# One core, hybrid streaming trunk: the gate tiles' last square and scaling taken apart, a plain load of h for tile 13, and other rings for the last pair

## The chip, the cores and the metric

The kernel runs on one core of a Trainium2 chip. The metric is device time in microseconds (us). "Before" is the median of three runs. A profiled execution stands beside it: it has its own time, and a span, which runs from its first to its last instruction. Times within the trace count from the start of the span.

## The reference, cut to what matters

One layer (DEPTH is 1) over 2048 prompt frames and 32 sample frames, D = 1024, all in float32:

```python
h = h + jnp.concatenate([yA, yB], axis=-1) @ w_out
gate = jax.nn.sigmoid(rmsnorm(h, g_ple) @ w_ple_gate)
h = h + (p @ w_ple) * gate
y = rmsnorm(h, g_final)
```

yA and yB come from one combined input projection (a gated short convolution and a pooling mixer). The change touches the last two lines alone: the gate's product with what is added to h, and the final norm.

## The kernel before

**Tiles and stages.** The frames are cut into 16 tiles of 128 rows (0 to 15) and one of 32 rows (16); NT is 17. Stage one makes yA and yB and writes them to memory. Stage two makes h = x + y W_out pair by pair and writes it to `h_d`; e = p W_ple of all tiles but the last prompt tile is made around its start and its end, and lies in `e_d`. Stage three, the gate stage, runs over the pairs of tiles (0, 1), (2, 3) ... (12, 13) in a loop (L1828), and then once over the last pair (14, 15) in a function of its own, `last_pair`. The text names a pair by its first tile: pair 12 is the tiles 12 and 13.

**A pair.** Each pair's product (256 rows by 1024 by 1024) is made by `seven` (L273), a Strassen-like scheme of seven half-size products instead of eight. Every half-size product is 12 matmuls on TensorE (PE), since each operand is split into two parts. Three PSUM banks X, Y, Z are used: X = A11 W11, then Y, then X goes on with S2 T2, Z = S1 T1, X goes on with S3 T3, Z goes on with S4 W22, X ends with A22 T4. Between these, `carry` copies a bank to SBUF on ScalarE (ACT), and `out` adds a bank to what was carried, on VectorE (DVE). A bank is written again only when its copy or its addition has been read out of it. `seven` calls steps 1 to 6 between the products, and whatever a step traces stands at that place in the program: step 1 after the first product, 2 after Y, 3 after S2 T2, 4 after S1 T1, 5 after S3 T3, 6 after the one that follows it. The last pair takes S4 W22 ahead of S3 T3, and ends with `end` (two halves of A22 T4, each of 256 columns, L1722).

**After the products.** `out` (L1576) makes the gate by a sigmoid on ACT (L1582, or L1579 for the last quarter), and multiplies e by it on DVE (L1584), a quarter at a time: (0,0), (1,1), (0,1), (1,0), the first figure being the tile of the pair, the second the half of its columns. Is there no h (`h is None`), then h is added by a transfer: GpSimd (POOL) issues a DMA from `h_d` that accumulates onto the tile e in SBUF (L1590), after (0,1) for the first tile and after (1,0) for the second. Then e holds the final h.

**The final norm of a tile** is `done_g` (L1594): a sum of squares on ACT (`sumsq`, L94), two small operations on POOL (L73, L77) that give the factor, a scaling by it and by g on DVE (L1597), and the store of 512 KB to the output (L1600; on POOL's queue up to tile 11, on SP's queue for the tiles 12 to 15). The tiles of a pair are finished in the next pair: the first tile in step 4, the second in step 6. For pair 12 that is in `last_pair`, steps 3 and 4. The last pair itself has h loaded plainly, adds on DVE (`gated`, L1640 and L1641) and norms by `square`, `weigh`, `root` and `normed`.

**What sets the order.** The tile framework orders each engine's instructions when it builds the program, by order in the program and by its own forecast of when their inputs are there; on the chip each engine and each DMA queue runs its list in that order. `keep_in_program_order` (in `last_pair`: `fixed`) pins an instruction behind the one of its engine that was traced just before it; others may still pass both. So the scaling of step 4 stands behind the instruction that VectorE had traced last before step 4.

**Buffers.** `ya` has 5 buffers of 512 KB: the e of every pair, and in the last pair also e of tile 14 and two tiles hg. `xh` has 4: the tiles hn (h turned, for the products of a pair, loaded by quarters) and the last pair's two h. `cmb` has 8: the split operands of the products, and in the last pair the four tiles wl, the weight of p W_ple for tile 15 (`chunk`, step 1), whose product is made inside the last pair (`second`, L109). A load waits until the last user of its buffer is done; for an e whose buffer held a finished tile that is the store of that tile.

Of the kernel before, what the change touches and what calls it, by code (L numbers as in the profile page):

```python
# [15 lines left out]
P = 128  # L16
# [12 lines left out]
NT = SEQ // P + 1  # L29
# [7 lines left out]
def trunk(ctx, tc, x_p, x_s, c_conv, c_pool, p_p, p_s, g_mix, w_in, conv_w, conv_b, pool_w,  # L37
# [8 lines left out]
    h_d = tc.dram_tile([T, D], F32, name="h_d")  # L46
    e_d = tc.dram_tile([T, D], F32, name="e_d")
# [44 lines left out]
    def sumsq(x, n, name, r=None, later=False):  # L92
        ssq = sm.tile([P, 1], F32, tag="ssq", name=f"ssq_{name}")
        ins = nc.scalar.activation(junk[:n], x[:n], AF.Square, accum_out=ssq[:n])  # L94
        if later:
            tc.keep_in_program_order(ins)
        return rstd_of(ssq, n, name, r)
# [295 lines left out]
    def load_rows(pool, name, i, pr, sa=None, queue=nc.sync):  # L393
        r, n = tiles[i]
        t = ring4(pool, f"{name}_{i}")
        queue.dma_start(t[:n], pr[r:r + n] if sa is None else rows_of(pr, sa, r, n))
        return t
# [906 lines left out]
    with ExitStack() as s2:  # L1304
        pool = lambda name, bufs: s2.enter_context(tc.tile_pool(name=name, bufs=bufs, reuse_waits="tile"))
        qa, xh, ya, cmb = (pool(*a) for a in (("qa", 2), ("xh", 4), ("ya", 5), ("cmb", 8)))
# [86 lines left out]
        S, W = {}, {}  # L1393
# [38 lines left out]
        for c in range(EARLY):  # L1432
            if c == EARLY - 2:
# [3 lines left out]
        st, ss = (s2.enter_context(tc.tile_pool(name=name, bufs=bufs, side="right", reuse_waits="tile"))  # L1437
                  for name, bufs in (("st", 4), ("ss", 3)))
# [64 lines left out]
        W = {}  # L1503
# [64 lines left out]
        def gate_ops(h, e, n, name, i):  # L1568
            scale = lambda at: rs_h[:n, i + at[0]:i + at[0] + 1]

            def carry(ps, at):
                t = st.tile([P, NH], F32, tag="t", name=f"c_{name}_{at[0]}{at[1]}")
                carried.append(nc.scalar.copy(t[:n], ps[:n]))  # L1573
                return t

            def out(ps, c, at):  # L1576
                if c is None:
                    c = st.tile([P, NH], F32, tag="t", name=f"g_{name}_{at[0]}{at[1]}")
                    nc.scalar.activation(c[:n], ps[:n], AF.Sigmoid, scale=scale(at))  # L1579
                else:  # L1580
                    nc.vector.tensor_tensor(c[:n], ps[:n], c[:n], op=ALU.add)
                    nc.scalar.activation(c[:n], c[:n], AF.Sigmoid, scale=scale(at))  # L1582
                ee = half_of(e, at, n)
                nc.vector.tensor_tensor(ee, ee, c[:n], op=ALU.mult)  # L1584
                if h is not None:
                    hh = half_of(h, at, n)
                    nc.vector.tensor_tensor(hh, hh, ee, op=ALU.add)
                elif at[0] + at[1] == 1:
                    r = tiles[i + at[0]][0]
                    nc.gpsimd.dma_start(e[at[0]], h_d[r:r + P], accum_op=ALU.add)  # L1590

            return carry, out

        def done_g(i, h, later=False):  # L1594
            r, n = tiles[i]
            rf = sumsq(h, n, f"f{i}", later=later)
            ins = nc.vector.scalar_tensor_tensor(h[:n], h[:n], rf[:n], g_bc[:n], op0=ALU.mult, op1=ALU.mult)  # L1597
            if later:
                tc.keep_in_program_order(ins)
            (nc.sync if NT - 5 <= i < NT - 1 else nc.gpsimd).dma_start(rows_of(y_p, y_s, r, n), h[:n])  # L1600
# [16 lines left out]

            return carry, out

        def last_pair(i, A, sooner, before):  # L1620

            pps = load_pps(ss.tile([P, 2, 2, P], F32R, tag="s", name="pps_l"), i + 1, nc.sync)
            e = load_rows(ya, "e", i, e_d)
            wp = []
            chunk = lambda: wp.extend(load_wp(cmb, "wl", nc.sync))

            h = [load_rows(xh, "h", i + b, h_d) for b in range(2)]
            tt = nc.vector.tensor_tensor
            carry, _ = gate_ops(h, [e], P, f"g{i}", i)
            hg = [ring4(ya, f"hg_{b}") for b in range(2)]
# [64 lines left out]
            def rest():  # L1699
                of_first(cols_of(0), nc.gpsimd)  # L1700
# [33 lines left out]
                weigh(1, cols_of(0))  # L1734
                normed(1, root(1))

            seven(f"g{i}", A, W, held, out, {1: chunk, 3: sooner, 4: lambda: (before(), rest()), 5: upper_half}, first_tile=True, end=end)

        def prep_g(i, ahead=False):

# [48 lines left out]
        S = {}  # L1789
        steps = prep_g(0)  # L1790
# [17 lines left out]
        def short_gate():  # L1808
# [7 lines left out]
            done_g(NT - 1, h)  # L1816
            yield

        def joined(a, b):
            def both(p, q):  # L1820
                def run():
                    p()
                    q()
                return run
            return {**a, **{st: both(a[st], f) if st in a else f for st, f in b.items()}}

        short_steps = short_gate()
        for i in range(0, NT - 3, 2):  # L1828
            A = S.pop(i)
            following = prep_g(i + 2, not i)  # L1830
            e = [load_rows(ya if i else xh, "e", i + b, e_d) for b in range(2)]
            if i:
                following = joined(following, finish)
            seven(f"g{i}", A, W, *gate_ops(None, e, P, f"g{i}", i), following)
            finish = {st: lambda b=b, i=i, e=e: done_g(i + b, e[b], True) for b, st in enumerate((4, 6))}
            if i in (0, 2, 4):
                next(short_steps)
        last_pair(NT - 3, S[NT - 3], finish[4], finish[6])

# [1 line left out]
_INS = ['x_prompt', 'x_sample', 'cache_conv', 'cache_pool', 'p_prompt', 'p_sample', 'g_mix', 'w_in',  # L1841
# [25 lines left out]
```

## Time and profile before

| what | us |
|---|---|
| median of 3 runs | 918.86 (917.51 to 918.87) |
| the profiled execution's own time | 916.35 |
| its span | 914.6 |
| TensorE busy, of the span | 890.8 (97%) |
| VectorE | 695.2 (76%) |
| ScalarE | 452.8 (50%) |
| GpSimd | 166.9 (18%) |
| mean granted TensorE clock | 0.995 |

How to read it: 1.75 us of the profiled execution's own time lie outside its span, and it was 2.51 us faster than the median. TensorE is busy nearly all of the time, so what counts is the idle time that is left on it and what ends each piece of it. In rows of the timeline the first number is the start, the second the length, then engine and line, `out<-in` by the program's names, and in brackets the engine's idle time before the row with what ended it. SPq and POOLq are the queues on which transfers are issued.

### The profile page before, as it was taken

To read this page: it belongs to the slowest core of one execution; us is meant where nothing else is said; L and a number is where in the kernel's file an instruction comes from. 1 tells how busy PE (TensorE), PEld (TensorE's weight loads), DVE (VectorE), ACT (ScalarE), POOL (GpSimd) and SP (SyncE) were. 2 spreads that over 40 slices of the span, in tenths; PEclk is the share of its full clock that TensorE was granted. 3 is DMA by queue.
4 is the path that set the end of the run, shared out by engine and by line. 5 is a ranking of instruction groups with operands and counts; after the bars stand their busy time and mean duration, and the time that the engine had idled before them with its cause. 6 is when DMAs were issued, how large, how long until landed. Compare 5 with 4: busy or idle time off the path is not lost. (4 is left out here: it accounts for less than half of the span.)

```text
span 914.6 us, 12059 instructions
## 1 busy us (share of the span) xinstructions
PE 890.8 (97%) x4110; PEld 718.0 (79%) x4110; DVE 695.2 (76%) x1138; ACT 452.8 (50%) x818; POOL 166.9 (18%) x304
## 2 busy tenths in 40 slices
PE   8999999999999999999999999999999999999995
PEld 6788888888888778877788886888887787768884
DVE  6899789897993788746677679956557967688874
ACT  7744555554443354433343375643435765446454
POOL 2210122222131123100000021211112201213322
PEclk9999999999999999999999999999999999999999
DMA  8155286856699676767754595878668774687975
GB/s 273 55 187 179 75 257 205 246 170 210 195 346 427 152 225 184 239 204 247 242 154 143 185 364 166 263 234 264 228 226 294 274 235 116 150 228 184 270 206 182
DMA packets 116843, 198.51 MB, mean 217 GB/s; under 512 B 13558, under 2 KB 74542, under 8 KB 115885
## 3 DMA queue, kind: packets, MB, share of 16 engines
q1 hardware_dynamic: 92749, 117.38, 40.9%
q0 software_dynamic: 21584, 75.96, 26.6%
q10 hardware_dynamic: 2448, 4.39, 1.3%
q8 instruction: 32, 0.52, 0.2%
q14 instruction: 30, 0.25, 0.1%
HBM read 132.53 MB, written 65.15 MB: 216 GB/s over the span
## 5 line engine op out<-in xcount | busy, mean ns | idle before, releaser
L185 PE MATMUL z_g<-wg,g_S 128*128 128x512 f32 x192 | 46.5, 391 | 1.0 <-ACT c_g L1573 1.0
L185 PE MATMUL z_o<-wo,y_S 128*128 128x512 f32 x192 | 47.4, 389 | 0.0
L646 PE MATMUL x_zab<-B,w_zab_S 128*128 128x512 f32 x192 | 46.8, 391 | 0.4 <-DVE w_zab_S L84 0.4
L185 PE MATMUL x_o<-wo_T,y_S 128*128 128x512 f32 x192 | 46.3, 390 | 0.9 <-DVE c_o L1319 0.9
L646 PE MATMUL z_zab<-B,w_zab_S 128*128 128x512 f32 x192 | 46.7, 390 | 0.0
L185 PE MATMUL x_o<-wo,y 128*128 128x512 f32 x192 | 45.2, 389 | 0.0
L185 PEld LDWEIGHTS z_g<-wg,g_S 128*128 128x128 f32 x192 | 35.8, 188 | 9.5 <-ACT c_g L1573 2.2
L646 PEld LDWEIGHTS x_zab<-B,w_zab_S 128*128 128x128 f32 x192 | 35.8, 188 | 9.1 <-DVE w_zab_S L84 0.9
L185 PEld LDWEIGHTS x_o<-wo_T,y_S 128*128 128x128 f32 x192 | 35.9, 188 | 8.7 <-DVE c_o L1319 1.3
L185 PEld LDWEIGHTS x_o<-wo,y 128*128 128x128 f32 x192 | 36.0, 188 | 7.7
L646 PEld LDWEIGHTS z_zab<-B,w_zab_S 128*128 128x128 f32 x192 | 35.8, 188 | 7.8 <-DVE w_zab_S L84 0.3
L185 PEld LDWEIGHTS z_o<-wo,y_S 128*128 128x128 f32 x192 | 36.0, 188 | 7.5
L646 PE MATMUL x_ch<-B,w_ch_S 128*128 128x512 f32 x168 | 41.9, 392 | 0.0
L646 PE MATMUL x_zbv<-B,w_zbv_S 128*128 128x512 f32 x168 | 40.9, 392 | 0.5 <-ACT zs L986 0.5
L646 PE MATMUL z_zbv<-B,w_zbv_S 128*128 128x512 f32 x168 | 40.4, 390 | 0.0
L646 PE MATMUL z_ch<-B,w_ch_S 128*128 128x512 f32 x168 | 40.4, 389 | 0.0
L646 PEld LDWEIGHTS x_zbv<-B,w_zbv_S 128*128 128x128 f32 x168 | 31.3, 188 | 8.3 <-ACT zs L986 1.0
L646 PEld LDWEIGHTS x_ch<-B,w_ch_S 128*128 128x128 f32 x168 | 31.3, 188 | 7.3 <-issue 0.4
L646 PEld LDWEIGHTS z_ch<-B,w_ch_S 128*128 128x128 f32 x168 | 31.5, 188 | 6.6
L646 PEld LDWEIGHTS z_zbv<-B,w_zbv_S 128*128 128x128 f32 x168 | 31.5, 188 | 6.5
L81 ACT CAST y_S<-y_fS 128x512 fp32r<-128x512 f32 x28 | 17.0, 620 | 26.7 <-PE x_o L185 11.9
L1373 POOL DMA_DIRECT2D gs<-in_w_ple_gate_dram x16 | 11.5, 716 | 88.2 <-DMA g_d<-gs 33.8
(554 smaller groups left out, 2275.1 us busy)
## 6 DMA issues: line engine op xcount, KB each, us to landing
wn<-in_w_in_dram SPq DMA_DIRECT2D x24, 512.0 KB, 4.7
hn<-h_d SPq DMA_DIRECT2D x65, 128.0 KB, 7.4
y<-y_d SPq DMA_DIRECT2D x16, 512.0 KB, 7.0
p_dT<-T POOLq DMA_DIRECT2D x15, 512.0 KB, 5.6
e<-e_d SPq DMA_DIRECT2D x15, 512.0 KB, 7.6
x<-in_x_prompt_dram SPq DMA_DIRECT2D x14, 512.0 KB, 5.9
e<-h_d POOLq DMA_DIRECT2D x14, 512.0 KB, 8.3
B<-p_d POOLq DMA_DIRECT2D x3, 2048.0 KB, 17.0
```

Of the source, the lines that this page charges most:

```text
L81: ins = nc.scalar.copy(hi, src)
L185: nc.tensor.matmul(ps[:n], lhs[:, k, a, :n], w[b][:, k], start=start and k + q == 0, stop=k == KH - 1 and q == 2, skip_group_check=True)
L646: nc.tensor.matmul(ps, lhs[:, k, x], b[:, k, y], start=start and k + q == 0, stop=stop and k == KH - 1 and q == 2, skip_group_check=True)
L1373: ins = nc.gpsimd.dma_start(t, rows[:, :, half * NH:half * NH + NH])
```

## The change

It has three parts. First, `done_g` can take a factor that is already there, and a new function `finishing` makes four steps of the two tiles' ends: square 0, scale 0, square 1, scale 1 (0 and 1 are the tiles of the pair that went before). In the pairs 2 to 12 they stand in the steps 4, 5, 5, 6 of the next pair; before, square and scaling together stood in 4 and 6. Second, pair 12 (`i == NT - 5`) loads h of tile 13, the fourteenth, plainly into a buffer of `xh`; `out` adds to it on VectorE, and the accumulating transfer is made for tile 12 alone. Third, the last pair takes the ends of pair 12 in another order: square 1 (tile 13) in step 1, scale 1 in step 2, square 0 (tile 12) in step 3, scale 0 in step 4; h of tile 15 comes into `ya` instead of `xh`, and e of tile 14 is asked for after both h instead of before.

```diff
-                if h is not None:
+                if h is not None and h[at[0]] is not None:
                     hh = half_of(h, at, n)
                     nc.vector.tensor_tensor(hh, hh, ee, op=ALU.add)
                 elif at[0] + at[1] == 1:
...
-        def done_g(i, h, later=False):
+        def done_g(i, h, later=False, rf=None):
             r, n = tiles[i]
-            rf = sumsq(h, n, f"f{i}", later=later)
+            rf = rf or sumsq(h, n, f"f{i}", later=later)
...
-        def last_pair(i, A, sooner, before):
+        def last_pair(i, A, square0, scale0, square1, scale1):
...
             pps = load_pps(ss.tile([P, 2, 2, P], F32R, tag="s", name="pps_l"), i + 1, nc.sync)
-            e = load_rows(ya, "e", i, e_d)
             wp = []
             chunk = lambda: wp.extend(load_wp(cmb, "wl", nc.sync))
 
-            h = [load_rows(xh, "h", i + b, h_d) for b in range(2)]
+            h = [load_rows(ya if b else xh, "h", i + b, h_d) for b in range(2)]
+            e = load_rows(ya, "e", i, e_d)
...
-            seven(f"g{i}", A, W, held, out, {1: chunk, 3: sooner, 4: lambda: (before(), rest()), 5: upper_half}, first_tile=True, end=end)
+            seven(f"g{i}", A, W, held, out, {1: lambda: (chunk(), square1()), 2: scale1, 3: square0, 4: lambda: (scale0(), rest()), 5: upper_half}, first_tile=True, end=end)
...
+        def finishing(i, out):
+            steps = []
+            for b in range(2):
+                rf = {}
+
+                def square(b=b, rf=rf):
+                    rf[0] = sumsq(out[b], P, f"f{i + b}", later=True)
+
+                def scale(b=b, rf=rf):
+                    done_g(i + b, out[b], True, rf[0])
+
+                steps += [square, scale]
+            return steps
...
             e = [load_rows(ya if i else xh, "e", i + b, e_d) for b in range(2)]
+            h = [None, load_rows(xh, "h", i + 1, h_d)] if i == NT - 5 else None
             if i:
-                following = joined(following, finish)
-            seven(f"g{i}", A, W, *gate_ops(None, e, P, f"g{i}", i), following)
-            finish = {st: lambda b=b, i=i, e=e: done_g(i + b, e[b], True) for b, st in enumerate((4, 6))}
+                for at, f in zip((4, 5, 5, 6), finish):
+                    following = joined(following, {at: f})
+            seven(f"g{i}", A, W, *gate_ops(h, e, P, f"g{i}", i), following)
+            finish = finishing(i, e if h is None else [e[0], h[1]])
             if i in (0, 2, 4):
                 next(short_steps)
-        last_pair(NT - 3, S[NT - 3], finish[4], finish[6])
+        last_pair(NT - 3, S[NT - 3], *finish)
```

## The prediction

> **What bounds the kernel now.** I read the page's first part, then what TensorE waited for in the gate stage, then busy time by stretches (columns: PE, PEld, DVE, ACT, POOL, granted clock, DMA share, GB/s).
>
> ```profile
> span 914.6 us, 12059 instructions
> PE 890.8 (97%) x4110; PEld 718.0 (79%) x4110; DVE 695.2 (76%) x1138; ACT 452.8 (50%) x818; POOL 166.9 (18%) x304
> ...
> PE x_gl L337 <- DVE c_gl L1608: 2.3, 1, 2.3
> PE x_g L1722 <- DVE c_g L1677: 2.0, 1, 2.0
> PE e L109 <- ACT eout L167: 2.0, 1, 2.0
> PE x_g L185 <- DVE c_g L1581: 1.4, 2, 0.9
> PE z_g L185 <- ACT c_g L1573: 1.0, 1, 1.0
> ...
> 843.00:862.40 19.40, 19.40 (x86) 15.76 (x85) 17.23 (x24) 11.50 (x20) 5.90 (x8) 1.00 1.04 264
> 862.40:881.70 19.30, 19.30 (x86) 15.68 (x85) 16.15 (x23) 10.47 (x19) 5.34 (x8) 1.00 0.78 228
> ```
>
> TensorE is the bound. In the pairs 10 and 12 (the two stretches) it is busy 19.40 of 19.40 and 19.30 of 19.30 us: there no other engine's work costs anything until it is late for a product. What the change can win is TensorE's idle time. Leaving out the 2.0 of e L109, which lies ahead of the pairs, the list sums to 2.3 + 2.0 + 1.4 + 1.0 = 6.7 us. Two of these waits stand in the last pair:
>
> ```profile
> 889.41 0.69 DVE L1640 TENSOR_TENSOR c_g<-e,c_g 128x512 f32<-128x512 f32 x1 [0.79 <-ACT c_g L1673]
> 890.14 0.69 DVE L1641 TENSOR_TENSOR h<-h,c_g 128x512 f32<-128x512 f32 x1
> 893.12 1.06 ACT L94 ACTIVATE junk<-e 128x1024 bf16<-128x1024 f32 x1 [2.26 <-DMA e<-h_d]
> 894.18 0.57 ACT L1573 COPY c_g<-z_g 128x512 f32<-128x512 f32 x1
> 894.80 3.01 PE L185 MATMUL z_g<-wg,g_S 128*128 128x512 f32 x12 [0.99 <-ACT c_g L1573]
> 896.90 1.06 ACT L94 ACTIVATE junk<-e 128x1024 bf16<-128x1024 f32 x1 [2.15 <-DMA e<-h_d]
> 899.00 1.29 DVE L1597 SCALAR_TENSOR_TENSOR e<-e,rstd_f,g_bc 128x1024 f32<-128x1024 f32 x1 [2.48 <-POOL rstd_f L77]
> 900.20 0.69 DVE L1677 TENSOR_TENSOR c_g<-z_g,c_g 128x512 f32<-128x512 f32 x1
> 899.47 1.52 PE L109 MATMUL e_l<-wl,pps_l 128*128 128x512 f32 x6
> ...
> 902.28 0.69 DVE L1677 TENSOR_TENSOR c_g<-x_g,c_g 128x512 f32<-128x512 f32 x1
> 903.02 1.69 PE L1722 MATMUL x_g<-wq,g 128*128 128x256 f32 x12 [2.04 <-DVE c_g L1677]
> ```
>
> The square of tile 12 (893.12) waits for its accumulating transfer; the copy of Z stands behind it, and TensorE loses 0.99. The square of tile 13 (896.90) waits likewise; its scaling (899.00) is ahead of the two readings of Z and X on VectorE, and TensorE loses 2.04. So 3.03 us hang on these two landings. The last scaling is what holds the end: Z is complete at 894.80 + 3.01 = 897.81, and is read at 900.20.
>
> **Part one, the steady pairs: about -0.4 us.** Squares and scalings are neither more nor fewer, and TensorE has no idle time in these pairs to give back: nothing there. Each scaling moves behind the (1,1) product of e, which comes after the reading of X that TensorE needs, so nothing is put ahead of that reading. Cover gone, it would cost a 1.28 us scaling at most. The one place where a scaling stands ahead of a wait of TensorE is the short tile's:
>
> ```profile
> 797.75 1.28 DVE L1597 SCALAR_TENSOR_TENSOR e<-e,rstd_f,g_bc 128x1024 f32<-128x1024 f32 x1 [0.44 <-POOL rstd_f L77]
> ...
> 801.70 1.14 PE L337 MATMUL x_gl<-wg,gl_a 128*64 128x512 f32 x4 [2.27 <-DVE c_gl L1608]
> ```
>
> With the square a product earlier the factor is there, and the 0.44 goes. Bounds: the whole 2.27, if ScalarE's earlier square lets L1608 move too; a loss of 1.28, if a scaling comes to stand where none was. I take the row, -0.44.
>
> **Part two, tile 13's h by VectorE.** Removed: one accumulating transfer on POOL's queue. Added: two additions of 0.69 (row 890.14 is the same form), and a plain load of h in SP's queue, which has a free buffer of `xh` and time until the first addition; at nothing, covered by pair 12's products. It also frees a buffer: e of tile 13 is done after the last addition. When is that?
>
> ```profile
> 881.06 1.28 DVE L1597 SCALAR_TENSOR_TENSOR e<-e,rstd_f,g_bc 128x1024 f32<-128x1024 f32 x1
> 881.16 1.04 ACT L94 ACTIVATE junk<-e 128x1024 bf16<-128x1024 f32 x1
> 882.26 1.29 DVE L1584 TENSOR_TENSOR e<-e,c_g 128x512 f32<-128x512 f32 x2
> 883.46 0.68 DVE L1584 TENSOR_TENSOR e<-e,g_g 128x512 f32<-128x512 f32 x1
> 883.85 0.90 POOL L1590 DMA_DIRECT2D e<-h_d  x1 [0.18 <-issue]
> 885.37 1.28 DVE L1597 SCALAR_TENSOR_TENSOR e<-e,rstd_f,g_bc 128x1024 f32<-128x1024 f32 x1 [1.23 <-POOL rstd_f L77]
> 887.93 0.69 DVE L1677 TENSOR_TENSOR c_g<-y_g,c_g 128x512 f32<-128x512 f32 x1 [1.27 <-PE y_g L185]
> ```
>
> From start to start a product takes 0.60 (two from 882.26 to 883.46) and a scaling 1.20 (881.06 to 882.26). The new order from 881.06: (1,1) product and addition, scaling of tile 10, (0,1) product, scaling of tile 11, (1,0) product and addition: 881.06 + 5 x 0.60 + 2 x 1.20 = 886.46. VectorE's next deadline is 887.93, so all of it lies in slack. Tile 12's accumulation starts after the (0,1) product, some 0.3 later than at 883.85. It held TensorE 0.99 before; 0.3 more there is hidden behind the later wait.
>
> **Part three, the last pair's rings: about +0.1 us, and the doubt of this forecast.** Tile 13's square no longer waits for a transfer: h is there at 886.5, its square ends near 888. But its scaling is pinned behind L1641 of the quarter (0,0), that one needs L1640, and L1640 needs e of tile 14. Here the rings count:
>
> ```profile
> 868.35 0.56 POOL L1600 DMA_DIRECT2D out_dram<-e  x1 [1.45 <-DVE e L1597]
> ...
> out_dram<-e POOLq DMA_DIRECT2D x1, 512.0 KB, 8.2
> ...
> 876.59 0.32 SPq L396 DMA_DIRECT2D e<-e_d  x1
> ```
>
> The store of tile 9 starts at 868.35 and lands 8.2 later, at 876.55; the load at 876.59, today e of tile 14, takes that buffer. Now h of tile 15, which is asked for first, takes it, though it is needed only after the reading of X at 902.28. Of the five buffers of `ya` that leaves e of tile 14 the first one to come free of those of the tiles 10 to 13: tile 13's, at about 886.5 (tile 10's store comes later). So a load that started at 876.59 starts ten microseconds later, in a busy stretch (last number of an issue row: us to landing):
>
> ```profile
> 882.51 8.03 SPq L123 DMA_DIRECT2D wl<-wl_d  x4
> ...
> 884.78 0.32 SPq L123 DMA_DIRECT2D wl<-wl_d  x1
> ...
> 887.50 0.32 SPq L123 DMA_DIRECT2D wl<-wl_d  x1
> ...
> wl<-wl_d SPq DMA_DIRECT2D x1, 512.0 KB, 4.0
> ...
> wl<-wl_d SPq DMA_DIRECT2D x1, 512.0 KB, 9.5
> ...
> wl<-wl_d SPq DMA_DIRECT2D x1, 512.0 KB, 9.3
> ...
> q0 software_dynamic: 204, 0.77, 67.1%
> q1 hardware_dynamic: 205, 0.77, 35.5%
> ```
>
> The landings are those of the first, third and fourth wl (882.51, 887.50 and, 0.32 before the four issues end at 890.54, 890.22); the last two rows are the queues from 888 to 894, POOL's q0 and SP's q1. SP's queue runs in order. At 886.5 the load of e comes between the second and the third wl. Early end: 4.0 after the start, 890.5, as the first wl. Late end in this place: the third wl's own landing, 887.50 + 9.5 = 897.0. I take the late rows, since the stretch is full: the mean of 886.5 + 9.5 = 896.0 and 897.0, so 896.5. The two wl behind it start no later than now, since their buffers come free after 886.5, but move back in the queue; their product (899.47, 1.52 long) can come up to 2.0 late before it delays the matmuls at 903.02.
>
> [...]
>
> VectorE then does L1640, L1641 and both scalings before it reads Z, since both scalings are pinned in that order: 0.73 (889.41 to 890.14), 0.61, 1.20, 1.20, together 3.74. 896.5 + 3.74 = 900.24, against 900.20 before. TensorE's wait of 2.04 thus keeps its size: the scaling that waited for an accumulation now waits for e. Every microsecond of e's landing is one of the end; the point of no change is 896.46.
>
> **Sum.** -0.44 + 0 + 0.04 = -0.40: 915.95 for the profiled execution's 916.35. That one was 2.51 below the median; on the median 918.46, so **918.5 us**, its own range 917.1 to 920.4 (landing of e from 895.5 to 898.4, the short tile's wait as it may).
>
> **The rivals.** *Faster, 915.4 to 917.* e of tile 14 is early enough: its load goes ahead of the second wl (884.78), or the stretch is lighter. For it: the stretch loses one transfer, and a landing by 897.81 - 3.74 = 894.1 is enough for VectorE to be ready when Z is. Against it: the buffer's 886.5. At such a landing the wait of 2.04 is gone: 916.35 - 2.04 - 0.44 + 2.51 = 916.4; with the copy of Z on time too, 0.99 less, 915.4. The short tile's 2.27 going whole gives the forecast 1.83 more, 916.6, alone. *Slower, 920.7 to 922.* The builder's forecast frees the buffer later than it frees those of wl, and the load of e stands behind the fourth wl: it then lands no sooner than 890.22 + 9.3 = 899.5. L1640 holds VectorE until then: 3.0 over the point of no change, 918.86 + 3.0 - 0.4 = 921.5. It decides from a landing of 898.7 on (918.86 + 1.84 + 0.4 over). For it: the third wl's buffer is free at 887.50, one microsecond after e's. *Nothing gained anywhere* (squares come sooner, TensorE waits as before) is 918.9, inside the forecast's range.
>
> **How the numbers follow.** Forecast, little change: 0.38. Faster rivals: 0.34 (e early 0.24, the short tile or the copy of Z 0.10). Slower: 0.28. 0.2% is 1.84 us, about what a measurement of this kernel tells from no change; the forecast's range lies all but inside it, the rivals outside. So faster 0.34, same 0.38, slower 0.28. The range takes in both rivals: 915.6 to 921.7 leaves out a tenth at each end.
>
> **What the profile after would show.** Right: the load of e of tile 14 near 886.5 in SP's queue, L1640 of the quarter (0,0) with a wait for that DMA of some 7 us, both scalings close behind it, Z read near 900.2, and L1722 idle about 2 us. Square of tile 13 before 889, with no wait for a DMA. Wrong: Z read before 898.5 and no wait ahead of L1722 (the faster rival), or L1640 held beyond 898.7 (the slower). In the pairs 8 to 12 TensorE should show no wait; one there would mean that a scaling came ahead of a reading of X. If the order on VectorE has the reading of Z ahead of L1640, the whole of part three falls.

## The result, and the profile after

The changed kernel took 910.58 us (median of 8 runs, 909.36 to 914.43), the kernel before 917.19 beside it (8 runs, 911.7 to 918.87): 0.9942 of before, 95% interval 0.9916 to 0.9968. Here it is faster by 0.6%, and below the forecast's 918.5 and its range from 915.6. Measured twice more (below) the change gave 0.9987 and 0.9985, with intervals that hold 1, so its size is less sure than its first interval says.

The changed kernel's page, first lines, and the list of what TensorE waited for (from the pairs on; us in total, times, longest):

```profile
span 911.4 us, 12057 instructions
PE 889.4 (98%) x4110; PEld 717.0 (79%) x4110; DVE 696.0 (76%) x1140; ACT 452.6 (50%) x818; POOL 166.8 (18%) x303
```

```profile
PE z_g L185 <- ACT c_g L1573: 2.1, 2, 1.7
PE x_g L185 <- DVE c_g L1581: 1.6, 2, 1.0
PE x_gl L337 <- DVE c_gl L1608: 1.0, 1, 1.0
PE x_g L1722 <- DVE c_g L1677: 0.2, 1, 0.2
```

The span is 3.2 shorter. The wait ahead of L1722 fell from 2.0 to 0.2, the short tile's from 2.3 to 1.0; the wait for the copy of Z (z_g) rose from 1.0 to 2.1 in two pieces, and its longer one stands in the last pair. Set side by side, matmul by matmul, the two traces are up to 0.9 apart in the earlier stages, which the change doesn't touch, and agree to 0.1 from 717 us to the short tile. By 806 us the changed kernel is 2.98 ahead, at the last pair's first matmul 2.25, at its z_g 1.6, and at L1722 3.37 (903.02 before, 899.65 after).

The short tile, after:

```profile
797.27 1.28 DVE L1597 SCALAR_TENSOR_TENSOR e<-e,rstd_f,g_bc 128x1024 f32<-128x1024 f32 x1
797.80 2.45 PE L185 MATMUL x_g<-wg,g 128*128 128x512 f32 x10
...
801.22 1.10 PE L337 MATMUL x_gl<-wg,gl_a 128*64 128x512 f32 x4 [0.97 <-DVE c_gl L1608]
```

And the one line before that answers to the second of these:

```profile
797.89 1.54 PE L185 MATMUL x_g<-wg,g 128*128 128x512 f32 x6
```

The scaling's 0.44 is gone, as forecast: TensorE goes on at 801.22 instead of 801.70. But TensorE also goes idle later, at 797.80 + 2.45 = 800.25 instead of 797.89 + 1.54 = 799.43: the planner (the tile framework, which orders every engine's instructions) has put ten matmuls of x_g ahead of x_gl, not six. So 1.30 of the wait is gone. The rest of the 2.98 is the clock. Stretches of two microseconds (start and end, length, busy times of five engines as in the prediction, then the granted clock), before:

```profile
802.00:804.00 2.00, 2.00 (x8) 0.92 (x7) 2.00 (x4) 0.01 (x1) 0.00 (x0) 0.65 1.08 342
804.00:806.00 2.00, 2.00 (x6) 1.58 (x5) 1.37 (x4) 0.58 (x1) 0.56 (x1) 0.50 0.96 194
```

and after:

```profile
802.00:804.00 2.00, 2.00 (x10) 1.31 (x9) 1.67 (x4) 0.65 (x2) 0.00 (x0) 1.00 1.02 280
804.00:806.00 2.00, 2.00 (x10) 1.67 (x9) 1.46 (x3) 1.75 (x3) 0.00 (x0) 1.00 0.93 155
```

TensorE counts as busy 2.00 of 2.00 in all four rows, yet does 8 and 6 matmuls before, 10 and 10 after: behind the long wait the granted clock fell to half (0.65 and 0.50 of full in these rows), behind the short one it did not (1.00).

The last pair, after:

```profile
882.28 0.91 POOL L1590 DMA_DIRECT2D e<-h_d  x1
884.52 0.32 SPq L396 DMA_DIRECT2D e<-e_d  x1
884.61 1.06 ACT L94 ACTIVATE junk<-h 128x1024 bf16<-128x1024 f32 x1 [1.49 <-DVE h L1587]
891.54 1.06 ACT L94 ACTIVATE junk<-e 128x1024 bf16<-128x1024 f32 x1 [2.98 <-DMA e<-h_d]
893.10 0.69 DVE L1640 TENSOR_TENSOR c_g<-e,c_g 128x512 f32<-128x512 f32 x1 [7.08 <-DMA e<-e_d]
893.22 3.02 PE L185 MATMUL z_g<-wg,g_S 128*128 128x512 f32 x12 [1.65 <-ACT c_g L1573]
895.63 1.28 DVE L1597 SCALAR_TENSOR_TENSOR e<-e,rstd_f,g_bc 128x1024 f32<-128x1024 f32 x1
896.83 0.68 DVE L1677 TENSOR_TENSOR c_g<-z_g,c_g 128x512 f32<-128x512 f32 x1
899.65 1.58 PE L1722 MATMUL x_g<-wq,g 128*128 128x256 f32 x11 [0.24 <-DVE c_g L1677]
```

The order is the one that was forecast: e of tile 14 asked for (884.52) when tile 13's last addition is done, square 1 without a transfer (884.61), L1640 held 7.08 by e, both scalings behind it, then the reading of Z. The times in it are not. From the pair's first matmul (880.07 here, 882.32 before) L1640 comes at 13.03, where the forecast's 896.5 is 14.18; and square 0 (891.54) comes at 11.47 instead of 10.81, so TensorE loses 1.65 for the copy of Z instead of 0.99.

### The profile page after: what moved, and what is told of

Its sections match the earlier page's. It is cut to its first block, busy times and chain, and to the rows that moved or that the text cites. A ratio compares the mean times of both kernels' runs of the same rounds, so it can differ in the third digit from the quotient of the medians.

```text
span 911.4 us, 12057 instructions
## 1 busy us (share of the span) xinstructions
PE 889.4 (98%) x4110; PEld 717.0 (79%) x4110; DVE 696.0 (76%) x1140; ACT 452.6 (50%) x818; POOL 166.8 (18%) x303
```

## The experiments

Every ratio is to the kernel before, measured beside it on the same chip, with its 95% interval. It is not the quotient of the two medians (copy_first's 914.93 has 0.9969, with before's median at 915.02), so a difference of some 0.002 between two ratios says little. Edits are against the changed kernel unless another is named. A table of the traces stands behind the last experiment.

**Both kernels once more.** Three runs without an edit.

> The kernel before, unchanged, timed against itself. Theory: the trace of the change is 3.14 us shorter as profiled (913.21 against 916.35), the medians 6.6 us apart (910.58 against 917.19), so single executions of one kernel differ by some us. This run should then give a ratio of 1 with an interval that holds it, and a trace whose waits are those of before: 2.27 ahead of the short tile's second product with a lower granted clock behind it, 0.99 ahead of z_g and 2.04 ahead of L1722 in the last pair. Rival: the waits and the low clock of that one trace were chance; then they differ here.

> The change as it is, on the same chip as the next two. Theory: 3 to 6.6 us faster than before, with TensorE's wait ahead of the short tile's second product near 1.0 and no lower clock behind it, 1.65 ahead of z_g and 0.24 ahead of L1722. Rival (the gain is that of single executions): under 2 us.

> The changed kernel once more. Its two sizes so far, 0.9942 (0.9916 to 0.9968) and 0.9987 (0.9963 to 1.001), differ by more than either interval likes. If the gain is made of waits that are shorter by 1.3 and 1.4 us and of a clock that falls to half behind long waits in some executions and not in others, the ratio lies between the two, about 0.997, with the mean clock of the runs no lower than before's. If the first was the size, it is under 0.995; if the second, above 0.998.

before_again: 914.58, 0.9995 (0.9975 to 1.0014). after_again: 913.67, 0.9987 (0.9963 to 1.001). after_third: 913.86, 0.9985 (0.996 to 1.001): by the bounds set for it, it sides with the second size, not with the 0.997 between the two; after_again's 0.0013, or 1.2 us, is its rival's size. before_again has before's waits (2.25, 0.67 and 2.10), but no half clock behind the first. Single executions of one kernel spread over 5 to 11 us. One thing that differs between them is shown by after_again's last pair:

```profile
883.71 0.91 POOL L1590 DMA_DIRECT2D e<-h_d  x1
894.23 1.06 ACT L94 ACTIVATE junk<-e 128x1024 bf16<-128x1024 f32 x1 [4.25 <-DMA e<-h_d]
895.91 4.59 PE L185 MATMUL z_g<-wg,g_S 128*128 128x512 f32 x12 [2.92 <-ACT c_g L1573]
```

The same order, but the accumulation lands 10.5 us after its issue instead of 9.3, TensorE waits 2.92, and the same twelve matmuls take 4.59 instead of 3.02, since the clock is at half behind the wait (granted 0.50 from 897 to 899 us).

Much of the spread arises ahead of all edits. Up to 774 us every engine and queue runs the same order in all 18 traces; yet TensorE's last matmul of e (`e<-wq,pps`, L109) ends anywhere from 728.81 us (e_copy) to 740.11 (after_third). Above all its wait near 716 us, mostly for a load of pps, ranges from none to 3.97, and in eleven traces has half clock behind it. Traces are better compared from there to the end of the span: 180.9 and 180.5 us in before and before_again; 177.8, 180.4 and 177.9 in the change's three; 178.4 in only4, 183.1 in not4, 177.4 in rest_4, 175.8 in rest_4_e and 175.6 in rest_4_e_copy (these five are described below).

**The change taken in two.** steps_only keeps the first part, rest_only the second and third.

In steps_only:

```diff
-            h = [load_rows(ya if b else xh, "h", i + b, h_d) for b in range(2)]
             e = load_rows(ya, "e", i, e_d)
+            h = [load_rows(xh, "h", i + b, h_d) for b in range(2)]
...
-            seven(f"g{i}", A, W, held, out, {1: lambda: (chunk(), square1()), 2: scale1, 3: square0, 4: lambda: (scale0(), rest()), 5: upper_half}, first_tile=True, end=end)
+            seven(f"g{i}", A, W, held, out, {1: chunk, 3: lambda: (square0(), scale0()), 4: lambda: (square1(), scale1(), rest()), 5: upper_half}, first_tile=True, end=end)
...
-            h = [None, load_rows(xh, "h", i + 1, h_d)] if i == NT - 5 else None
+            h = None
```

In rest_only:

```diff
-                for at, f in zip((4, 5, 5, 6), finish):
+                for at, f in zip((4, 4, 6, 6), finish):
```

steps_store has steps_only's edits, and tile 11's store on SP's queue:

```diff
-            (nc.sync if NT - 5 <= i < NT - 1 else nc.gpsimd).dma_start(rows_of(y_p, y_s, r, n), h[:n])
+            (nc.sync if NT - 6 <= i < NT - 1 else nc.gpsimd).dma_start(rows_of(y_p, y_s, r, n), h[:n])
```

> Part one alone: squares and scalings in the steps 4, 5, 5, 6 of the pairs 2 to 12; the last pair and pair 12 as before. Theory of two places: the short tile's wait falls from 2.27 to about 1.0 and the lower clock behind it goes, together about 2.9 us; the last pair keeps its 0.99 and 2.04; 2.4 to 2.9 us faster than before. Rival, as forecast (only the 0.44 goes): about 0.4 faster. Rival that all of the gain is the last pair's: no difference.

> Parts two and three alone: tile 13's h by VectorE, the last pair's order and rings; squares and scalings of the other pairs together in the steps 4 and 6 as before. Theory of two places: 2.04 ahead of L1722 falls under 0.5, the wait ahead of z_g grows to about 1.6; about 1.1 us faster than before, with the short tile's wait and low clock still there. Rival, as forecast (e of tile 14 late enough to eat all): no difference. Rival that all of the gain is the last pair's: 3 us or more.

> Part one alone, as in steps_only, but the store of tile 11 is issued on SP's queue instead of POOL's. In steps_only that store (883.78) came ahead of tile 13's accumulation (884.39) on POOL's queue, which then landed 16.8 us after the last pair's first matmul, against 14.5 before, and L1722 waited 4.56 instead of 2.04. Theory: with the store off that queue the accumulation lands about 14.5 again, L1722 waits about 2, and the kernel is 2 us or more faster than steps_only, level with before or somewhat faster. Rival (the accumulation is late because it is issued later, or by chance): L1722 still waits 4 or more.

steps_only: 917.66, 1.0035 (1.0016 to 1.0054), slower than before, which none of its three cases had. rest_only: 914.6, 0.9995 (0.9971 to 1.0019): no gain, as its first rival had it. Its two waits are not those of its theory (1.19 ahead of L1722, 0.51 ahead of z_g): without the split the accumulation starts as early as before. steps_store: 914.25, 0.9981 (0.9956 to 1.0006). steps_only's short tile waits only 0.81, and its loss is in the last pair:

```profile
883.78 0.56 POOL L1600 DMA_DIRECT2D out_dram<-e  x1 [0.32 <-DVE e L1597]
884.39 0.85 POOL L1590 DMA_DIRECT2D e<-h_d  x1
...
898.04 1.06 ACT L94 ACTIVATE junk<-e 128x1024 bf16<-128x1024 f32 x1 [4.70 <-DMA e<-h_d]
904.16 2.07 PE L1722 MATMUL x_g<-wq,g 128*128 128x256 f32 x8 [4.56 <-DVE c_g L1677]
```

Since tile 11's scaling has passed the last product of pair 12, its store (883.78) stands on POOL's queue ahead of tile 13's accumulation (884.39), which lands 13.6 us later. With that store on SP's queue, in steps_store, the same accumulation lands 2.4 us sooner after the pair's first matmul and L1722's wait is back at before's size:

```profile
883.36 0.34 SPq L1600 DMA_DIRECT2D out_dram<-e  x1
884.23 0.85 POOL L1590 DMA_DIRECT2D e<-h_d  x1 [0.92 <-DVE e L1584]
...
901.62 2.87 PE L1722 MATMUL x_g<-wq,g 128*128 128x256 f32 x12 [2.06 <-DVE c_g L1677]
```

So the split alone loses in the last pair more than it wins at the short tile, unless that store leaves the queue or, as the change has it, that accumulation does.

**The last pair's two waits.** Which transfer sets its end in the changed kernel, e of tile 14 or tile 12's accumulation?

In e_first:

```diff
+            e = load_rows(ya, "e", i, e_d)
             h = [load_rows(ya if b else xh, "h", i + b, h_d) for b in range(2)]
-            e = load_rows(ya, "e", i, e_d)
```

In copy_first (e_copy has both edits):

```diff
-            seven(f"g{i}", A, W, held, out, {1: lambda: (chunk(), square1()), 2: scale1, 3: square0, 4: lambda: (scale0(), rest()), 5: upper_half}, first_tile=True, end=end)
+            seven(f"g{i}", A, W, held, out, {1: lambda: (chunk(), square1()), 2: scale1, 4: lambda: (square0(), scale0(), rest()), 5: upper_half}, first_tile=True, end=end)
```

In e_late, where e's buffer is taken without its load:

```diff
-            chunk = lambda: wp.extend(load_wp(cmb, "wl", nc.sync))
+            def chunk():
+                wp.extend(load_wp(cmb, "wl", nc.sync))
+                tc.keep_in_program_order(nc.sync.dma_start(e, e_d[i * P:i * P + P]))
...
-            e = load_rows(ya, "e", i, e_d)
+            e = ring4(ya, f"e_{i}")
```

both_plain has e_first's edit, and both tiles of pair 12 get a plain h:

```diff
-            seven(f"g{i}", A, W, held, out, {1: lambda: (chunk(), square1()), 2: scale1, 3: square0, 4: lambda: (scale0(), rest()), 5: upper_half}, first_tile=True, end=end)
+            seven(f"g{i}", A, W, held, out, {1: lambda: (chunk(), square0(), square1()), 2: lambda: (scale0(), scale1()), 4: rest, 5: upper_half}, first_tile=True, end=end)
...
-            h = [None, load_rows(xh, "h", i + 1, h_d)] if i == NT - 5 else None
+            h = [load_rows(xh, "h", i + b, h_d) for b in range(2)] if i == NT - 5 else None
...
-            finish = finishing(i, e if h is None else [e[0], h[1]])
+            finish = finishing(i, e if h is None else h)
```

> The change, with e of tile 14 asked for ahead of both h again; h of tile 15 takes the buffer that comes free late. Theory: VectorE's wait of 7.1 us ahead of L1640 goes, the scaling of tile 13 comes some 4 us sooner; but the scaling of tile 12 still waits for its square, and that for the accumulation, so Z's reading comes at most 1 us sooner and TensorE's wait ahead of z_g (1.65 and 2.92 in two traces of the change) stays: within 1 us of the change. Rival, as forecast (every microsecond of e's landing is one of the end): 2 us or more faster than the change.

> The change, with the square of tile 12 traced in step 4, behind the copy of Z instead of ahead of it. Theory: the wait ahead of z_g, 1.65 to 2.92, goes whole (the copy follows Z's product at once) and with it the lower clock that one trace showed behind it; the end is then held by e of tile 14 alone, so a wait of up to 2 us comes back ahead of L1722; 0 to 2 us faster than the change. Rival (the square's landing is what ends last): no difference, with L1722 waiting as much more as z_g waits less.

> The changed kernel with both of the last pair's remaining waits attacked: e of tile 14 is asked for ahead of the two h (which takes e's landing off VectorE's path), and square 0 stands a step later, behind the copy of Z on ScalarE (which takes tile 12's accumulation off that copy). Each alone gave 0.997 of before, as each left the other's wait. Theory (the two waits are separate and add up): no wait over 0.5 us ahead of z_g or of L1722, the last pair 1 to 2 us shorter than in the change, the time 3 to 5 us under before's. Rival (tile 12's accumulation is the one price, and goes to whatever stands behind it): z_g without a wait, but square 0 waits for the accumulation until 894 to 895 and scale 0 holds the reading of Z, so that L1722 waits 1 to 3 us and the time is that of the change or up to 1 us over it.

> The changed kernel, with one thing put off: the load of e of tile 14 is pinned behind the four loads of wl on SP's queue. The prediction's chain says that every microsecond of its landing past the one that VectorE can hide is one of the end. Expected by it: issue 5 to 6 us later than in the change (there 4.5 us after the pair's first matmul), landing 18 to 20 us after the pair's first matmul instead of 12.9, L1640 waiting for that transfer, Z read as much later as 3.7 us behind the landing, and TensorE's wait ahead of L1722 (0.24 in the change) 4 to 6 us; the time 4 to 6 us over the change's, and over before's by 1 to 4. Rival (e's landing is not the price, the accumulation of tile 12 is): the wait ahead of L1722 stays under 1, the time within 1 us of the change's.

> The change, with h of tile 12 loaded plainly as well (no accumulating transfer in pair 12), e of tile 14 asked for first, both squares of pair 12 in step 1 and both scalings in step 2. Theory: no transfer stands on the last pair's path any more: no wait ahead of z_g and under 0.3 ahead of L1722, 1.5 to 3 us faster than the change, 3 to 5 faster than before. Rival (the plain loads come as late as the accumulations did, since all share the same stretch): waits of 1 us or more for h of tile 14 on VectorE, and no gain over the change.

e_first: 914.32, 0.9973 (0.9949 to 0.9996). copy_first: 914.93, 0.9969 (0.9945 to 0.9993). e_copy: 912.31, 0.9964 (0.9942 to 0.9986). e_late: 915.35, 0.9986 (0.9965 to 1.0007). both_plain: 913.38, 0.998 (0.9956 to 1.0003). In e_first L1640 no longer waits for e, and TensorE waits for the accumulation:

```profile
892.42 1.06 ACT L94 ACTIVATE junk<-e 128x1024 bf16<-128x1024 f32 x1 [3.96 <-DMA e<-h_d]
894.10 4.56 PE L185 MATMUL z_g<-wg,g_S 128*128 128x512 f32 x12 [2.63 <-ACT c_g L1573]
```

In copy_first z_g does not wait, and e holds the end:

```profile
897.78 0.69 DVE L1640 TENSOR_TENSOR c_g<-e,c_g 128x512 f32<-128x512 f32 x1 [7.53 <-DMA e<-e_d]
...
904.32 1.70 PE L1722 MATMUL x_g<-wq,g 128*128 128x256 f32 x12 [2.51 <-DVE c_g L1677]
```

In e_copy z_g does not wait and e is early, and the time is the theory's; but the accumulation (square 0 at 888.35, 12.66 after the pair's first matmul) still holds scaling 0 and so L1722:

```profile
888.35 1.06 ACT L94 ACTIVATE junk<-e 128x1024 bf16<-128x1024 f32 x1 [1.40 <-DMA e<-h_d]
...
894.47 1.69 PE L1722 MATMUL x_g<-wq,g 128*128 128x256 f32 x12 [1.22 <-DVE c_g L1677]
```

e_late (its lines from 1640 on are two higher) misses what I had expected, 4 to 6 us over the change:

```profile
890.45 1.01 SPq L1630 DMA_DIRECT2D e<-e_d  x1
896.06 4.60 PE L185 MATMUL z_g<-wg,g_S 128*128 128x512 f32 x12 [2.78 <-ACT c_g L1573]
...
898.29 0.69 DVE L1642 TENSOR_TENSOR c_g<-e,c_g 128x512 f32<-128x512 f32 x1 [10.55 <-DMA e<-e_d]
902.02 0.68 DVE L1679 TENSOR_TENSOR c_g<-z_g,c_g 128x512 f32<-128x512 f32 x1
902.34 2.24 PE L109 MATMUL e_l<-wl,pps_l 128*128 128x512 f32 x12
902.62 0.68 DVE L1679 TENSOR_TENSOR c_g<-x_g,c_g 128x512 f32<-128x512 f32 x1
904.41 1.60 PE L1724 MATMUL x_g<-wq,g 128*128 128x256 f32 x12
```

e lands 3.5 later than in the change (16.50 after the pair's first matmul, not 13.03) and L1724 waits for nothing. The accumulation, and the half clock behind its wait, had already put Z back to 896.06 + 4.60 = 900.66; Z is read 1.4 after that, and the products of tile 15 in between cover it. That does not show that a later e is free. With the change's 3.02 for z_g, Z would have been complete at 899.08. And the edit moved more than the load: the planner has X read right behind Z (902.62; in the change's trace L1640 of the next quarter stands between them, with Z at 896.83 and X at 898.91), and twelve matmuls of tile 15 ahead of L1724 instead of six. L1724 comes 22.62 after the pair's first matmul, 3.0 later than in the change's first trace and 0.6 later than in after_again, which had the half clock too. What the three experiments show is that Z is read when two things are there: Z itself, which the accumulation holds back, and VectorE, which e holds back; the later one counts. both_plain, which has no accumulation left in pair 12, pays with waits of 1.85 and 1.12 on TensorE inside pair 12 and the last pair, and gains nothing over the change. Ahead of the first, VectorE had waited 5.96 for a load of hn; why that one comes late stays open.

**The split in one pair alone.** only4 is the kernel before with squares and scalings taken apart in pair 4 only, the pair in which the short tile's product stands; not4 is the complement, the changed kernel without the split in pair 4.

only4 has steps_only's edits (the last pair as before) and this one:

```diff
-                for at, f in zip((4, 5, 5, 6), finish):
+                for at, f in zip((4, 5, 5, 6) if i == 4 else (4, 4, 6, 6), finish):
```

In not4:

```diff
-                for at, f in zip((4, 5, 5, 6), finish):
+                for at, f in zip((4, 4, 6, 6) if i == 4 else (4, 5, 5, 6), finish):
```

> The kernel before, with squares and scalings taken apart in one pair alone: the pair 4, whose steps end the pair 2 just ahead of the short tile's pair 4 work. All else, the last pair too, is as before. Theory (about a third to a half of the gain is made at the short tile): TensorE's wait ahead of x_gl (L337) is about 1.0 instead of 2.2 to 2.3, no stretch of half clock follows it, and the last pair keeps waits of about 1 ahead of z_g and 2 ahead of L1722; the time is 1 to 3 us under before's. Rival (the short tile's shorter wait was an accident of that one trace, or is made up for later): the wait stays above 2, or it is 1.0 and the time is within 0.5 us of before's.

> The changed kernel, but in pair 4 alone square and scaling stand together in 4 and 6 as before: the complement of only4 and of rest_4. Theory: the short tile's wait is back at 2.2 to 2.3, with half clock behind it in part of the executions, and the last pair is the change's (accumulation at 2.21, z_g waiting 1.6 to 2.9): the time 1.3 to 2.9 us over the change's, within 1 us of before's. Rival (the short tile is worth nothing): the time is the change's.

only4: 912.99, 0.997 (0.9949 to 0.9992), with one changed place in the whole kernel. Matmul by matmul, its trace gains 2.97 on before's between 721 and 806 us, of which 2.46 are left at the end: the gain is made at the short tile. not4: 917.97, 1.0021 (1.0 to 1.0043), where the change gave 0.9942, 0.9987 and 0.9985: without the short tile's part nothing of the gain is left. Their x_gl rows, only4 first:

```profile
798.55 1.11 PE L337 MATMUL x_gl<-wg,gl_a 128*64 128x512 f32 x4 [0.90 <-DVE c_gl L1608]
```

```profile
803.02 1.94 PE L337 MATMUL x_gl<-wg,gl_a 128*64 128x512 f32 x4 [2.48 <-DVE c_gl L1608]
```

In not4 the clock is at half again behind the wait (granted 0.50 from 804 to 806 us; four matmuls in 1.94 instead of 1.11).

**The split kept out of all pairs but pair 4.** rest_4 is the changed kernel with the split in pair 4 only, so it is out of the pairs 2, 6, 8, 10 and 12; rest_4_e and rest_4_e_copy add e_first's and then copy_first's edit.

```diff
-                for at, f in zip((4, 5, 5, 6), finish):
+                for at, f in zip((4, 5, 5, 6) if i == 4 else (4, 4, 6, 6), finish):
```

> The changed kernel, but square and scaling stand taken apart only in the ends that pair 4 carries (steps 4, 5, 5, 6); in all other pairs they stand together again in 4 and 6. Theory: the split helps at the short tile alone and harms in pair 12, where it puts the start of tile 12's accumulation 0.68 us back (2.21 instead of 1.53 after the last pair's first matmul, in seven traces against five). So: short tile's wait about 1.0, accumulation issued at 1.53, square 0 at 10.3 to 10.8, z_g waiting 0.5 to 1.0 instead of 1.65 to 2.9, L1722 at 19.4 after the pair's first matmul; the time 1 to 3 us under the change's, 0.995 to 0.997 of before. Rival (the accumulation lands when the two queues let it, wherever it starts): square 0 at 11.5 to 12.7 as in the change, time as the change's.

> As rest_4, with e of tile 14 asked for ahead of the two h. Theory: with the accumulation landing at 10.3 to 10.8 its wait ahead of z_g is 0.5 to 1.0, and with e early L1640, L1641 and scale 1 are done before Z is, so L1722 waits under 0.5: it comes 18.2 to 18.7 us after the pair's first matmul, against 20.5 to 20.8 before and 19.6 to 20.0 in the change. Time 0.994 to 0.996 of before. Rival (the wait is only moved on): L1722 waits 1 to 2 and the time is that of rest_4.

> As rest_4_e, with square 0 a step later, behind the copy of Z. Theory: no wait ahead of z_g (the copy stands ahead of the square), the square at 10.5 to 11.0 and scale 0 before Z is complete at 14.3, so L1722 without a wait at 17.5 to 18.0: the shortest last pair of all, 0.993 to 0.995 of before. Rival: the accumulation is as late as in e_copy (12.66), L1722 waits 1.2 and the gain over e_copy is nothing.

rest_4: 910.16, 0.9949 (0.9927 to 0.9971). rest_4_e: 909.6, 0.9937 (0.9914 to 0.9961). rest_4_e_copy: 908.9, 0.9924 (0.9895 to 0.9952; 6 runs), the lowest of all, though the three intervals overlap. The three traces came as their theories had it, to some 0.2 us, and the times a little lower. In rest_4 the accumulation starts at 1.53 after the pair's first matmul again, lands 8.9 later, and both waits are small:

```profile
878.15 0.90 POOL L1590 DMA_DIRECT2D e<-h_d  x1 [0.19 <-issue]
887.01 1.06 ACT L94 ACTIVATE junk<-e 128x1024 bf16<-128x1024 f32 x1 [1.89 <-DMA e<-h_d]
888.68 3.02 PE L185 MATMUL z_g<-wg,g_S 128*128 128x512 f32 x12 [0.57 <-ACT c_g L1573]
896.11 1.70 PE L1722 MATMUL x_g<-wq,g 128*128 128x256 f32 x12 [1.23 <-DVE c_g L1677]
```

In rest_4_e_copy both waits are gone, and TensorE is busy from the pair's first matmul to L1722, 17.30 of 17.30 us (timeline, then the stretch):

```profile
891.91 1.06 ACT L94 ACTIVATE junk<-e 128x1024 bf16<-128x1024 f32 x1
892.13 2.95 PE L185 MATMUL z_g<-wg,g_S 128*128 128x512 f32 x12
898.09 1.66 PE L1722 MATMUL x_g<-wq,g 128*128 128x256 f32 x12
```

```profile
880.80:898.10 17.30, 17.30 (x78) 14.06 (x76) 10.96 (x16) 6.90 (x13) 8.13 (x11) 1.00 0.91 304
```

**The traces side by side** (without steps_only, steps_store and both_plain, whose pair 12 is built otherwise). TensorE's wait ahead of x_gl; then, counted from the last pair's first matmul, the issue of tile 12's accumulation and the start of square 0; TensorE's waits ahead of z_g and L1722; and L1722 itself, with a star where the clock fell to half between the two.

| kernel | x_gl | issue | square 0 | z_g | L1722 waits | L1722 at | ratio |
|---|---|---|---|---|---|---|---|
| before | 2.27 | 1.53 | 10.81 | 0.99 | 2.04 | 20.70 | 1 |
| before_again | 2.25 | 1.53 | 10.49 | 0.67 | 2.10 | 20.45 | 0.9995 |
| only4 | 0.90 | 1.53 | 10.81 | 0.99 | 2.13 | 20.80 | 0.9970 |
| rest_only | 2.19 | 1.53 | 10.33 | 0.51 | 1.19 | 19.42 | 0.9995 |
| the change | 0.97 | 2.21 | 11.47 | 1.65 | 0.24 | 19.58 | 0.9942 |
| after_again | 0.66 | 2.21 | 12.74 | 2.92 | 0 | 22.01* | 0.9987 |
| after_third | 0.87 | 2.21 | 12.19 | 2.37 | 0 | 19.96 | 0.9985 |
| not4 | 2.48 | 2.21 | 12.46 | 2.64 | 0 | 21.73* | 1.0021 |
| e_first | 0.79 | 2.21 | 12.45 | 2.63 | 0 | 21.71* | 0.9973 |
| copy_first | 0.90 | 2.21 | 12.50 | 0 | 2.51 | 20.03 | 0.9969 |
| e_copy | 0.94 | 2.21 | 12.66 | 0 | 1.22 | 18.79 | 0.9964 |
| e_late | 1.05 | 2.21 | 12.60 | 2.78 | 0 | 22.62* | 0.9986 |
| rest_4 | 0.82 | 1.53 | 10.39 | 0.57 | 1.23 | 19.49 | 0.9949 |
| rest_4_e | 0.90 | 1.53 | 10.62 | 0.80 | 0 | 18.32 | 0.9937 |
| rest_4_e_copy | 0.94 | 1.53 | 11.11 | 0 | 0 | 17.29 | 0.9924 |

## Why the prediction was wrong

**What held.** TensorE is the bound. That only its idle time was to be won did not hold: 1.68 of the 2.98 at the short tile was lost in time in which it counts as busy, at half clock. The buffers, the order on VectorE and on SP's queue, and what waits for what came as derived: tile 13's last addition done 4.42 us after the last pair's first matmul (forecast 886.46 - 882.32 = 4.14), e of tile 14 between the second and the third wl, L1640 with 7.08 for that DMA where some 7 was forecast, both scalings close behind it. SP's queue ran in order, as the forecast took it: in the changed kernel's trace none of the 131 transfers on it whose landing is shown landed ahead of one issued before it, and a wl, e and the next wl, issued at 880.26, 884.52 and 885.25, landed 3.4, 8.5 and 9.5 later.

**Part one, the failed step: "I take the row, -0.44".** The row was right about VectorE (0.48 sooner). It was wrong to stop there, in two ways. The planner orders TensorE too, and with the scaling earlier it put four more matmuls ahead of the wait; the wait's beginning moved as well as its end, 1.30 together. And the wait of 2.27 had a price behind it: the matmuls after it ran at half clock in before's trace, 2.98 in all (in three of the four traces with a wait of 2.19 to 2.48 there; not in before_again). By itself the split in pair 4 is worth 0.003 of 916 us, some 2.7 us (only4; 0.7 to 4.7 by its interval). The prediction had the whole 2.27 as a bound and gave it, together with the copy of Z, a chance of 0.10.

**Part one, "nothing there" for the steady pairs.** With the split everywhere a wait of 0.41 to 0.47 ahead of z_g stands near 836 us, in pair 8 (0.45 in the changed kernel, 0.47 in after_again, 0.43 in e_first); before, only4 and rest_4 have none there. It is not a scaling ahead of a reading of X, the sign that the forecast named: the copy of Z comes late on ScalarE, where five casts now stand ahead of it.

**Part two, a second failed step: "some 0.3 later ... hidden behind the later wait".** The accumulation of tile 12 starts 0.68 later. The prediction's own steps give 0.60, since the addition of 0.60 stands ahead of the product that releases it; I compared a product's end with an issue. And it was not hidden: it landed 9.3 to 10.5 after its issue in the eight traces with 2.21, 8.8 to 9.3 in six where it starts at 1.53 and the square waits for it, so that square 0 is 0.7 to 1.9 later than in before's own trace. The later wait that was to hide it had all but gone with e's landing. Putting the split out of all pairs but pair 4 (rest_4 against the change, 0.9949 against 0.9985 to 0.9987) gives back some 3 us by the two later measurements of the change, nothing by the first (0.9942), and 0.5, 3.0 and 0.5 in the traces from e's last matmul on; in rest_4's trace square 0 is at 10.39. The wait of 0.45 in pair 8 is part of that; what pair 12's split costs alone was not measured. Why the transfer itself takes longer from that start stays open.

**Part three, mechanism right, size wrong.** The term that was mis-sized is e's landing. e of tile 14 held L1640 until 13.03, 13.67 and 13.41 after the pair's first matmul in the change's three traces, not 14.18: in the first that is 8.6 us after its issue, where I had taken 10.0. The chain behind it held. By "every microsecond of e's landing is one of the end" L1722 comes as much ahead of before's 20.70 as L1640 comes ahead of the point of no change, 896.46 - 882.32 = 14.14. That gives 19.59 for the change's first trace, and 19.58 was measured; in after_third, rest_only, rest_4 and copy_first it fits to 0.02 as well (L1640 at 13.41, 12.87, 12.94 and 13.48). So of the 2.04 ahead of L1722 some 1.1 was won by e, and nearly all of the rest had only moved to z_g. What the chain lacked is the case in which Z itself comes later than e's path: then e no longer counts. In after_again z_g waits 2.92, with half clock behind it, and L1722 comes at 22.01 instead of 20.23; in e_first e is early and L1722 still comes at 21.71. I had looked at the two landings one behind the other, as they were before; the change runs both into the same place, and the later path counts. The load of e landed 8.5 us after its issue, 1.0 sooner than the late row's 9.5; whether the transfer taken off POOL's queue did that is not shown, since e's place in SP's queue differs too.

**The sum.** The time came out 7.9 under the forecast. Of this the short tile is some 2.3 more than the -0.44, by only4. The last pair is 1.1 less in the first trace (20.70 to 19.58), but longer in after_again: there the change gives back at z_g what it wins at L1722. And the level was too high: I started from the median of three runs, 918.86, while before's eight runs beside the change have 917.19, and its 133 runs in the four later measurements medians of 915.0 to 915.9. Against the two later measurements of the change the forecast's ratio of 0.9996 is off by about 0.001, less than they can tell; that would be luck, since the terms in it were wrong and cancelled. Against the first, 0.9942, it is off by 0.0054. Which of the two the change is worth is not settled. By differences of ratios, each sure to some 2 to 3 us only, its parts are: a gain of some 2.7 at the short tile (only4), of 0.4 (rest_only) to 1.9 (rest_4 against only4) by the last pair's rings and the plain h, and a loss of up to 3 by the split in the other pairs.

The faster rival named both gains but priced each alone, at 915.4 to 916.6. No case had the two together, and the range ended at 915.6.

## What to carry to other kernels

A reordering is worth what the planner makes of it on every engine: read which matmuls stand ahead of a wait, not only what ends it. Apply a change at the place that pays and nowhere else (the split in pair 4 alone beat the split everywhere by some 3 us against two of three measurements, and with it the last pair's other two edits took L1722 from 19.49 to 18.32 and 17.29 instead of trading waits). Where two paths feed one end, the later one sets it, and taking away either alone only moves the wait. Compare traces from the point where the edits begin: ahead of it single executions of this kernel differ by up to 11 us.

## What the runs showed of the hardware

In these traces half clock followed most waits of TensorE of about two microseconds or more. In the 18 traces of this case TensorE waited 30 times for more than 1.9 us after the first 100 us, and in 22 of them the granted clock was at half during the wait or within 4 us behind it; of 73 waits between 0.8 and 1.9 us, in one. The wait was 2.0 to 2.9 us in 19 of the 22. Every such stretch of half clock lasted 3.41 us (in before from 717.29 and from 802.62), or twice that (e_late and steps_only, once each), and the twelve matmuls in after_again took 1.57 us longer in it (4.59 against 3.02). The same wait was not always followed by it: 2.27 in before was, 2.25 in before_again was not. Such a stretch in after_again:

```profile
895.00:897.00 2.00, 1.09 (x3) 0.90 (x4) 1.80 (x3) 1.10 (x4) 1.43 (x2) 0.73 0.86 350
897.00:899.00 2.00, 2.00 (x6) 1.58 (x5) 1.97 (x2) 0.48 (x2) 1.36 (x2) 0.50 0.24 96
```

Executions of one kernel differ along with their clock: over 326 executions of these kernels, the time within a kernel rises by 0.94 us for each 0.001 that the mean granted clock is lower, which accounts for some 45% of the variance.

At the same time of issue, 3.27 us after the pair's first matmul, a store of 512 KB ahead of an accumulation on POOL's queue, and not on SP's, put the latter's landing back by 2.4 us (the square that waits for it starts 16.92 after that matmul in steps_only, 14.54 in steps_store; one trace each).
